# Gates and lifting products by rows, a compressor with moving weights, and a rank for the work beside the large products

## The chip, the core and the metric

The kernel runs on one core of a Trainium2 chip. The metric is the device time of one execution in microseconds (us). TensorE is PE here (its weight loads are PEld), VectorE is DVE, ScalarE is ACT, GpSimd is POOL, and SyncE is SP, which issues the loads from memory.

## What is computed

Two transformer blocks in a row on 256 tokens of width 1024, all in float32. The first block has four branches (a gated delta rule, a spatial gate, a sliding window attention, an attention over a memory), whose outputs are lifted to 1024, gated, added and projected:

```python
    ys = jnp.stack([y_a, y_b, y_c, y_m], axis=2)
    proj = jnp.einsum("btnc,ncd->btnd", ys, w_up)
    gates = jax.nn.sigmoid(gate_logits.reshape(B, T, N_BRANCH, D))
    merged = jnp.sum(gates * proj, axis=2)
    out = merged @ w_out
    return x + _rmsnorm(out, norm_post)
```

The second block has two layers. Each adds half a gated FFN (hidden size 2816), a mixer (MLA in layer 0, NSA in layer 1) and another half FFN, each behind an RMS norm of its own. The NSA mixer has a compressor: keys and values of 15 overlapping blocks of 32 tokens, in 4 groups, go through a small two-layer net.

```python
def compress_blocks(x, blk_idx, pos_emb, w1, w2):
    blocks = x[:, blk_idx] + pos_emb[None, None, :, None, :]
    flat = jnp.moveaxis(blocks, 3, 2).reshape(B, n_cmp, x.shape[2], L * x.shape[3])
    return jax.nn.gelu(flat @ w1) @ w2
```

## The kernel before

Tokens stand in two tiles of 128, called t = 0 and t = 1. Every large product is made of three fp32r matmuls: both factors are split into a high and a low part (`wh`, `wl` for weights, `xTh`, `xTl` or `yTh`, `yTl` for activations), and high x high, high x low and low x high are added in one PSUM bank. `mm3` (L236) issues the three. Weights come from memory as `raw` (SP, L211 and L214), and ACT and DVE split them (L220, L221).

There are two forms. In `ts` and `Product` (L308, L269) a 128 x 128 block of x stands in PE and the weights move, 512 columns at a time; the output has tokens as its rows. In `ws` (L315) a block of weights stands and x moves, 256 columns (all tokens) at a time; the output has features as its rows, which is the layout that a following product wants. `ws2` (L329) is a variant used by the FFNs. A factor whose rows are tokens has to be transposed first: `split_T` (L400) queues transposes on PE (L394) and the split of their result on ACT and DVE (L415, L416).

The small work is spread between the large matmuls. Transposes stand in a list `pending`, and attention, the delta rule and the compressor are generators in a list `beside`. After every large matmul `drip()` (L147) calls `step()` (L151), which issues one item of either. `wait` or `lag` items of nothing ahead of a norm's transposes (`LAG_NORM` = 28, `LAG_HIDDEN` = 20) leave time for the norm, whose own chain (square on ACT, two POOL operations for `rstd`, `xn` on DVE at L441) is written under `high_priority(100)`.

The order on each engine isn't the order of the code. The framework's scheduler takes instructions by priority, which is their place in the code minus the offset of a `high_priority` around them, among those that are ready in a timing of its own. Engines then execute their lists in order.

The merge stage (L1043 to L1085) runs the four branches one after the other. For each branch and each half of the 1024 columns, a `ws` product makes the gate (tanh on ACT, L1070) and a `ws` product lifts the branch; DVE multiplies and adds into `merged`, whose rows are features, and in the last branch `split` writes the high and low parts `moT` directly. `w_out` is then a `Product` on `moT`, and its evacuation ends in the norm that feeds the first FFN.

The compressor (L1491 to L1541) handles K and then V. It loads w1 as one tile of 1 MB, adds the position embedding (L1508), and issues 16 matmuls with w1 standing and 60 columns moving (L1513); then gelu and a second layer (L1528 and after), which gives `kcT` and `vbd` for the attention over compressed blocks.

Of the kernel before, what the change touches and what calls it, by code (L numbers as in the profile page):

```python
# [17 lines left out]
P = 128  # L18
# [75 lines left out]
def two_blocks_kernel(ctx: ExitStack, tc: tile.TileContext, a, cst_dram, cst2_dram, out):  # L94
# [51 lines left out]

    def drip():  # L147
        for _ in range(pace[0]):
            step()

    def step():  # L151
        f = pending.pop(0) if pending else None
        if f:
            f()
        elif beside:
            g = beside.pop(0)
            try:
                next(g)
                beside.append(g)
            except StopIteration:  # L160
                pass

    def idle(n):
        for _ in range(n):
            yield
# [362 lines left out]
    def first(nxt):  # L528
# [516 lines left out]
        merged = pg.tile([P, 8, T], F32)  # L1045
# [9 lines left out]
        for at, (br, name) in enumerate([(1, "b"), (2, "c"), (0, "a"), (3, "m")]):  # L1055
# [11 lines left out]
            for n in range(2):  # L1067
                gate = pg.tile([P, 4, T], F32, name="gate", bufs=1)
                ws(xT, 8, w_in, 0, 5896 + br * D + n * 512, 512,
                   lambda j0, w, pv, gate=gate: sc.activation(gate[:, j0:j0 + w, :], pv, AF.Tanh, scale=0.5))  # L1070
                if at == 3:
                    moT.append(ypair())

                def ev(j0, w, pv, n=n, gate=gate, at=at):
                    g, m = gate[:, j0:j0 + w, :], merged[:, 4 * n + j0:4 * n + j0 + w, :]
                    if at == 0:
                        ve.scalar_tensor_tensor(m, g, 1.0, pv, op0=OP.add, op1=OP.mult)
                    else:
                        ve.scalar_tensor_tensor(g, g, 1.0, pv, op0=OP.add, op1=OP.mult)
# [25 lines left out]
        in_turns([(pr, u) for u in range(4)], await_second=False)  # L1105
# [312 lines left out]
    def nsa(xn, nxt, skew):  # L1418
# [72 lines left out]
        def compress():  # L1491
            for which in range(2):
                s = "kv"[which]
                w1 = pk.tile([P, 16, P], F32, name="w1")
                nc.sync.dma_start(w1, a[f"nsa_cmp_w1_{s}_2"][0].rearrange("(k p) n -> p k n", p=P))
                w2 = pk.tile([P, P], F32, name="w2" + s)
                for b in range(2):
                    nc.sync.dma_start(w2[:, b * 64:(b + 1) * 64], a[f"nsa_cmp_w2_{s}_2"][0])
                pos = pk.tile([16, P], F32, name="pos" + s)
                nc.sync.dma_start(pos, a[f"nsa_cmp_pos_{s}_2"][0].rearrange("(j b) d -> j (b d)", b=2))  # L1500
                ps = tr()
                pe.transpose(ps[:, :16], pos, ident[:16, :16])
                posT = pk.tile([P, 16], F32, name="posT" + s)
                ve.tensor_copy(posT, ps[:, :16])
                c2 = c2s[which]
                fl = pk.tile([P, 16, 60], F32, name="flat")
                for j in range(16):
                    ve.tensor_scalar(fl[:, j, :].rearrange("p (g n) -> p g n", g=4), c2[:, :, 2 * j:2 * j + 225:16],  # L1508
                                     posT[:, j:j + 1], None, op0=OP.add)
                yield from idle(4)  # L1510
                ps = po()
                for j in range(16):
# [3 lines left out]
                hx = pk.tile([P, 60], F32, name="hx", bufs=2)  # L1516
                ve.tensor_copy(hx, ps[:, :60])
                hd = pk.tile([P, 4, 4, 32], F32, name="hid")
                gp.memset(hd, 0.0)
                h2 = pk.tile([P, 60], F32, name="h2", bufs=2)  # L1520
                gelu2(h2, hx, pk, 64)
                ve.tensor_scalar(hd[:, :, :, 0:15],
                                 h2.rearrange("p (g n) -> p g n", g=4)[:, :, None, :].to_broadcast([P, 4, 4, 15]),
                                 0.5, None, op0=OP.mult)
                yield from idle(16)
                ps = po()
                if which == 0:
                    pe.matmul(ps[:, :P].rearrange("p (g n) -> p g n", g=4), w2, hd[:, :, 0, :], start=True, stop=True)  # L1528
                    for b in range(2):
                        bs = slice(64 * b, 64 * b + 64)  # L1530
                        ve.tensor_copy(kcT[bs, :, b, 0:15], ps[bs, :P].rearrange("p (g n) -> p g n", g=4)[:, :, 0:15])
                else:
                    for g in range(4):
                        pe.matmul(ps[:, g * 64:(g + 1) * 64], hd[:, g].rearrange("p r n -> p (r n)"), w2[:, 0:64],
                                  start=True, stop=True)
# [212 lines left out]
```

## Time and profile before

| what | value |
|---|---|
| median of 3 runs | 1414.67 us (1414.62 to 1415.38) |
| profiled execution | 1415.39 us, span 1413.6 us |
| granted TensorE clock, mean | 0.999 |
| PE busy | 1387.0 us (98%) |
| PEld busy | 1208.0 us (85%) |
| DVE busy | 927.3 us (66%) |
| ACT busy | 733.3 us (52%) |
| POOL busy | 45.8 us (3%) |

A busy time is the time in which an engine has at least one instruction in work. Matmuls overlap in the pipeline of PE, so the length of a record is longer than the distance from one start to the next; what PE pays for a matmul is that distance. The stages follow each other: the first block's branches until some 250 us, its merge stage until some 396, FFN 0a until 595, MLA until 700, FFN 0b until 890, FFN 1a until 1075, NSA until 1225, FFN 1b until the end.

### The profile page before, as it was taken

The page shows a single profiled execution, that of the slowest core. Times are in us where ns is not written, and L with a number is a line of the kernel's source. Part 1 is how long each engine was busy: PE and PEld are TensorE (multiplying, and loading weights), DVE is VectorE, ACT ScalarE, POOL GpSimd, SP SyncE. Part 2 cuts the span into 40 slices and gives each one's busy share as a digit, 9 for nine tenths or more (in the row PEclk, how much of TensorE's full clock was granted, in tenths as well). Part 3 has the DMA queues.
Part 4 walks back from the last instruction along what each step waited for, and adds up shares of the span by engine and source line. Part 5 has one row for each costly group of instructions (what it writes and reads, how often), then busy time and mean ns, then how long its engine had stood idle before and what let it go on. Part 6 is the DMA issues. An engine that isn't in the chain of part 4 may idle for free.

```text
span 1413.6 us, 21329 instructions
## 1 busy us (share of the span) xinstructions
PE 1387.0 (98%) x8528; PEld 1208.0 (85%) x8528; DVE 927.3 (66%) x1587; ACT 733.3 (52%) x1293; POOL 45.8 (3%) x87
## 2 busy tenths in 40 slices
PE   7999999999999999999999999999999999999998
PEld 6998989999978888888788888888888887788886
DVE  6878666555667665669666656666665687576654
ACT  6646454343445454567454545555445467464543
POOL 1003000000010000010000000000000000000000
PEclk9999999999999999999999999999999999999999
DMA  7425634455556565533477664666556730465651
GB/s 259 149 83 166 222 126 150 149 179 180 179 164 208 182 202 183 174 116 122 140 229 258 197 208 150 200 202 197 190 188 207 203 80 31 134 207 182 200 186 60
DMA packets 172537, 241.77 MB, mean 171 GB/s; under 512 B 5264, under 2 KB 121749, under 8 KB 172309
## 3 DMA queue, kind: packets, MB, share of 16 engines
q1 hardware_dynamic: 172436, 240.40, 53.3%
q8 instruction: 67, 1.10, 0.3%
q14 instruction: 34, 0.27, 0.1%
HBM read 239.31 MB, written 4.22 MB: 172 GB/s over the span
## 4 chain that ended last, share of the span: by engine, by line
PE 86%; DMA 4%; ACT 4%; DVE 3%; POOL 1%; issue 1%; SPq 0%; POOLq 0%; ACTq 0%; DVEq 0%
PE acc L347 17%; PE acc L241 10%; PE acc L237 10%; PE acc L239 10%; PE acc L350 9%; PE d L241 5%; PE d L237 5%; PE d L239 5%; PE tr L394 4%; DVE wl L221 2%; ACT wh L220 1%; DMA raw<-in_ffn_b_w_gate_dram 1%; ACT pr L1582 1%; PE po L789 1%; DMA raw<-in_ffn_b_w_up_dram 1%
## 5 line engine op out<-in xcount | busy, mean ns | idle before, releaser
L221 DVE TENSOR_TENSOR wl<-raw,wh 128x1024 fp32r<-128x1024 f32 (+5 forms) x434 | 509.7, 1197 | 224.7 <-ACT wh L220 222.9
L220 ACT CAST wh<-raw 128x1024 fp32r<-128x1024 f32 (+5 forms) x434 | 433.8, 1029 | 308.0 <-PE d L241 95.1
L347 PE MATMUL acc<-xT,wh 128*128 128x512 f32 x1152 | 399.0, 397 | 1.5 <-DVE up L355 1.5
L350 PE MATMUL acc<-xT,wl 128*128 128x256 f32 x1152 | 298.9, 280 | 0.0
L347 PEld LDWEIGHTS acc<-xT,wh 128*128 128x128 f32 x1152 | 208.1, 188 | 43.4 <-DVE up L355 2.3
L350 PEld LDWEIGHTS acc<-xT,wl 128*128 128x128 f32 x1152 | 217.1, 188 | 12.1
L239 PE MATMUL acc<-xT,wh 128*128 128x256 f32 x544 | 156.6, 288 | 0.0
L241 PE MATMUL acc<-xT,wl 128*128 128x256 f32 x544 | 156.3, 287 | 0.0
L237 PE MATMUL acc<-xT,wh 128*128 128x256 f32 x544 | 156.1, 287 | 0.0
L241 PE MATMUL d<-wh,yTl 128*128 128x512 f32 x352 | 138.0, 392 | 0.0
L237 PE MATMUL d<-wh,yTh 128*128 128x512 f32 x352 | 137.6, 391 | 0.0
L239 PE MATMUL d<-wl,yTh 128*128 128x512 f32 x352 | 137.5, 391 | 0.0
L239 PEld LDWEIGHTS acc<-xT,wh 128*128 128x128 f32 x544 | 104.2, 192 | 1.1 <-issue 0.8
L237 PEld LDWEIGHTS acc<-xT,wh 128*128 128x128 f32 x544 | 104.2, 191 | 0.7 <-DVE y_b L481 0.3
L241 PEld LDWEIGHTS acc<-xT,wl 128*128 128x128 f32 x544 | 104.2, 191 | 0.4 <-issue 0.2
L237 PE MATMUL acc<-wh,xT 128*128 128x512 f32 (+4 forms) x256 | 97.4, 381 | 0.3 <-ACT xT L415 0.3
L239 PE MATMUL acc<-wl,xT 128*128 128x512 f32 (+4 forms) x256 | 96.2, 376 | 0.0
L241 PE MATMUL acc<-wh,xT 128*128 128x512 f32 (+4 forms) x256 | 96.0, 377 | 0.0
L241 PEld LDWEIGHTS d<-wh,yTl 128*128 128x128 f32 x352 | 66.1, 188 | 14.9 <-DVE yTl L1151 0.8
L239 PEld LDWEIGHTS d<-wl,yTh 128*128 128x128 f32 x352 | 66.1, 188 | 14.1
L237 PEld LDWEIGHTS d<-wh,yTh 128*128 128x128 f32 x352 | 66.1, 188 | 13.1
L354 ACT COPY sg<-acc 128x256 f32<-128x256 f32 x72 | 26.8, 373 | 89.2 <-PE acc L347 88.7
(436 smaller groups left out, 2034.6 us busy)
## 6 DMA issues: line engine op xcount, KB each, us to landing
raw<-in_w_in_dram SPq DMA_DIRECT2D x37, 1024.0 KB, 5.2
raw<-in_ffn_a_w_gate_dram SPq DMA_DIRECT2D x22, 1024.0 KB, 5.3
raw<-in_ffn_a_w_up_dram SPq DMA_DIRECT2D x22, 1024.0 KB, 5.3
raw<-in_ffn_a_w_down_dram SPq DMA_DIRECT2D x22, 1024.0 KB, 5.0
raw<-in_ffn_b_w_gate_dram SPq DMA_DIRECT2D x22, 1024.0 KB, 5.3
raw<-in_ffn_b_w_up_dram SPq DMA_DIRECT2D x22, 1024.0 KB, 5.3
raw<-in_ffn_b_w_down_dram SPq DMA_DIRECT2D x22, 1024.0 KB, 5.0
raw<-in_w_up_dram SPq DMA_DIRECT2D x8, 1024.0 KB, 5.0
```

Of the source, the lines that this page charges most:

```text
L220: sc.copy(h[:, c], raw[:, c])
L221: ve.tensor_sub(l[:, c], raw[:, c], f32(h[:, c]))
L237: pe.matmul(ps, ah, bh, start=start, stop=False)
L239: pe.matmul(ps, ah, bl, start=False, stop=False)
L241: pe.matmul(ps, al, bh, start=False, stop=stop)
L347: pe.matmul(ps, h[:, k, js], pair.both(kk), start=k == 0, stop=k == nk - 1)
L350: pe.matmul(ps[:, :T], l[:, k, js], pair[0][:, kk, :], start=False, stop=False)
L354: sc.copy(d, ps[:, T:])
L394: pe.transpose(box[0][:m, b * P:(b + 1) * P], src(b), ident)
L789: pe.matmul(p[:, h * 64:(h + 1) * 64], Em[:, h, :], Vs[t][:, h, :], start=True, stop=True)
L1582: sc.activation(p[:, sl], p[:, sl], AF.Exp, bias=nm[:, e:e + 1], scale=-1.0, accum_out=sm[:, e:e + 1])
```

## The change

It has three parts. `step()` runs under `high_priority(offset=60)`, so each small instruction that it issues ranks 60 places ahead of where the code has it. The merge's gates and lifting products use `ts` instead of `ws`: `merged` has tokens as its rows, and in the last branch it goes through `split_T`, with its transposes on PE; `w_out` waits for them (`await_second` is left at True). The compressor treats K and V together: its input stands (64 columns, 4 groups of 16) and w1 moves, 128 wide, K into the lower and V into the upper half of the rows of one bank; w1 comes in four chunks for each of K and V, from two buffers each; gelu is done once for both, and one transpose of `h2` gives the second layer's inputs.

```diff
+    rank = [60]
...
     def step():
-        f = pending.pop(0) if pending else None
-        if f:
-            f()
-        elif beside:
...
+        with tc.high_priority(offset=rank[0]):
+            f = pending.pop(0) if pending else None
+            if f:
+                f()
+            elif beside:
...
-        merged = pg.tile([P, 8, T], F32)
+        merged = pg.tile([P, 2, D], F32)
...
-                gate = pg.tile([P, 4, T], F32, name="gate", bufs=1)
-                ws(xT, 8, w_in, 0, 5896 + br * D + n * 512, 512,
-                   lambda j0, w, pv, gate=gate: sc.activation(gate[:, j0:j0 + w, :], pv, AF.Tanh, scale=0.5))
+                gate = pg.tile([P, 2, 512], F32, name="gate", bufs=1)
+                ts(xT, 8, w_in, 0, 5896 + br * D + n * 512, 512,
+                   lambda t, p, gate=gate: sc.activation(gate[:, t, :], p, AF.Tanh, scale=0.5))
...
-                        split(m, [v[:, j0:j0 + w, :] for v in moT[n]])
-
-                ws(yT, 4, a["w_up"][0, br], 0, n * 512, 512, ev)
+                        split_T(m, 4, [moT[n]], t, wait=LAG_HIDDEN)
+
+                ts(yT, 4, a["w_up"][0, br], 0, n * 512, 512, ev)
...
-                mo = merged.rearrange("p k t -> p (k t)")[:, t * D + m * 512:t * D + (m + 1) * 512]
+                mo = merged[:, t, ns]
...
-        in_turns([(pr, u) for u in range(4)], await_second=False)
+        in_turns([(pr, u) for u in range(4)])
...
-                w1 = pk.tile([P, 16, P], F32, name="w1")
-                nc.sync.dma_start(w1, a[f"nsa_cmp_w1_{s}_2"][0].rearrange("(k p) n -> p k n", p=P))
...
-                for j in range(16):
-                    pe.matmul(ps[:, :60], w1[:, j, :], fl[:, j, :], start=j == 0, stop=j == 15)
-                    if j % 2:
-                        yield
...
+            hidden = po()
+            for j0 in range(0, 16, 4):
+                w1, fl = [], []
+                for which in range(2):
+                    x = "kv"[which]
+                    w1.append(pk.tile([P, 4, P], F32, name="w1" + x, bufs=2))
+                    nc.sync.dma_start(w1[which], a[f"nsa_cmp_w1_{x}_2"][0, j0 * P:(j0 + 4) * P].rearrange(
+                        "(k p) n -> p k n", p=P))
...
                 yield from idle(4)
...
+                for i in range(4):
+                    for which in range(2):
+                        pe.matmul(hidden[64 * which:64 * which + 64, :P], fl[which][:, i].rearrange("p g n -> p (g n)"),
+                                  w1[which][:, i, :], start=j0 + i == 0, stop=j0 + i == 15)
+                    yield
...
+            gelu2(h2, hx, pk, P)
+            yield from idle(16)
+            ps = tr()
+            pe.transpose(ps[:, :P], h2, ident)
+            hk = pk.tile([P, 64], F32, name="hk")
+            ve.tensor_scalar(hk, ps[:, 0:64], 0.5, None, op0=OP.mult)
```

In the instruction lists this shows as follows. Up to the merge, a line of the kernel before stands 3 lines further down in the changed one (L394 becomes L397, L237 becomes L240).

The first place is PE at the end of FFN 0a. `d_4348` (before) and `d_3792` (after) are the two banks whose end starts the norm of token tile 0, and `tr<-cst,xn` are the transposes of its result. Before, with all but the first and the last of the 29 matmuls in between left out:

```order
L241 MATMUL d_4348<-wh,yTl 128x512
L237 MATMUL d_4349<-wh,yTh 128x512
...
L239 MATMUL d_4350<-wl,yTh 128x512
L394 MATMUL tr<-cst,xn 128x128
L241 MATMUL d_4350<-wh,yTl 128x512
L394 MATMUL tr<-cst,xn 128x128
L237 MATMUL d_4350<-wh,yTh 128x512
```

After, with 12 matmuls in between, of which the first and the last are shown:

```order
L244 MATMUL d_3792<-wh,yTl 128x512
L240 MATMUL d_3793<-wh,yTh 128x512
...
L244 MATMUL d_3794<-wh,yTl 128x512
L397 MATMUL tr<-cst,xn 128x128 x4
L240 MATMUL d_3793<-wh,yTh 128x512
L397 MATMUL tr<-cst,xn 128x128 x4
L242 MATMUL d_3793<-wl,yTh 128x512
```

The transposes have moved 17 matmuls ahead and stand in two groups of four.

The second place is PE at the end of the merge, where the last lifting product passes into `w_out` (banks `po`). Before:

```order
L239 MATMUL acc<-yTl,wh 128x256
L241 MATMUL acc<-yTh,wl 128x256
L237 MATMUL po<-wh,yTh 128x512
L239 MATMUL po<-wl,yTh 128x512
L241 MATMUL po<-wh,yTl 128x512
```

After:

```order
L244 MATMUL acc<-wh,yTl 128x512
L397 MATMUL tr<-cst,merged 128x128 x4
L240 MATMUL po<-wh,yTh 128x512
L242 MATMUL po<-wl,yTh 128x512
L244 MATMUL po<-wh,yTl 128x512
L240 MATMUL po<-wh,yTh 128x512
L242 MATMUL po<-wl,yTh 128x512
L397 MATMUL tr<-cst,merged 128x128 x4
```

The lifting matmuls are 512 wide, and the two groups of transposes of `merged` stand inside the first matmuls of `w_out`; two more groups stand in the same way after the first half.

The third place is SP in front of NSA's last products, where the chunks of w1 are queued. Before:

```order
L211 DMA raw<-in_nsa_w_o_dram 64x2x1024 x3
L1495 DMA w_10502<-in_nsa_cmp_w_v_dram 128x16x128
L211 DMA raw<-in_nsa_w_o_dram 64x2x1024 x5
L214 DMA raw<-in_ffn_b_w_gate_dram 128x4x512 x2
L214 DMA raw<-in_ffn_b_w_up_dram 128x4x512 x2
```

After:

```order
L214 DMA raw<-in_nsa_w_o_dram 64x2x1024 x3
L1515 DMA w1k<-in_nsa_cmp_w_k_dram 128x4x128
L1515 DMA w1v<-in_nsa_cmp_w_v_dram 128x4x128
L1515 DMA w1k<-in_nsa_cmp_w_k_dram 128x4x128
L1515 DMA w1v<-in_nsa_cmp_w_v_dram 128x4x128
L214 DMA raw<-in_nsa_w_o_dram 64x2x1024 x5
```

Chunks 2 and 3 of K and V stand where the load of V's w1 stood; chunks 0 and 1 are loaded in FFN 0b.

## Rows read from the trace of the kernel before

**Rows 1.** The page: busy time of each engine; the granted clock in 40 slices.

```profile
PE 1387.0 (98%) x8528; PEld 1208.0 (85%) x8528; DVE 927.3 (66%) x1587; ACT 733.3 (52%) x1293; POOL 45.8 (3%) x87
...
PEclk9999999999999999999999999999999999999999
```

**Rows 2.** PE's waits: line, releaser; us in total, times, longest us.

```profile
PE tr L394 <- DVE xn L441: 13.3, 6, 8.8
PE acc L347 <- DVE up L355: 1.5, 2, 1.3
```

**Rows 3.** Busy time by window, the merge stage: length, PE, PEld, DVE, ACT, POOL, clock, DMA.

```profile
250.00:396.00 146.00, 146.00 (x1169) 143.75 (x1168) 81.68 (x86) 61.59 (x74) 0.00 (x0) 1.00 0.55 174
```

**Rows 4.** Timeline of PE (start, length): 256-wide and 512-wide matmuls.

```profile
255.02 0.28 PE L237 MATMUL acc<-xT,wh 128*128 128x256 f32 x1
...
261.98 0.28 PE L239 MATMUL acc<-xT,wh 128*128 128x256 f32 x1
...
155.26 0.39 PE L241 MATMUL acc<-wh,xT 128*128 128x512 f32 x1
...
165.47 0.39 PE L241 MATMUL acc<-wh,xT 128*128 128x512 f32 x1
```

**Rows 5.** Timeline of PE at NSA's end: transposes of `xn` in groups of four.

```profile
1226.47 0.63 PE L394 MATMUL tr<-cst,xn 128*128 128x128 f32 x4 [1.03 <-DVE xn L441]
...
1227.17 0.60 PE L394 MATMUL tr<-cst,xn 128*128 128x128 f32 x4
```

**Rows 6.** Timeline of PE: the compressor's V, and the attention's pairs with 64-column weights.

```profile
1129.15 3.68 PE L1513 MATMUL wo<-flat,w 128*128 128x60 f32 x32
...
1147.39 0.44 PE L1600 MATMUL wo<-pT,vs 128*64 128x128 f32 x4 [0.16 <-ACT pT L504]
...
1147.98 0.30 PE L1622 MATMUL mm<-kcT,qT 128*128 128x32 f32 x1
```

**Rows 7.** SP's load of V's w1, and DMA issues (KB each, us to landing).

```profile
1121.52 0.74 SPq L1495 DMA_DIRECT2D w<-in_nsa_cmp_w_v_dram  x1
...
w<-in_nsa_cmp_w_v_dram SPq DMA_DIRECT2D x1, 0.5 KB, 6.9
```

**Rows 8.** Timeline at the end of FFN 0a: the norm's chain and its transposes.

```profile
585.27 0.39 PE L241 MATMUL d<-wh,yTl 128*128 128x512 f32 x1
...
585.69 0.69 DVE L1170 SCALAR_TENSOR_TENSOR res<-d,res 128x512 f32<-128x512 f32 x1 [2.03 <-PE d L241]
...
586.48 0.63 ACT L371 ACTIVATE junk<-res 128x512 bf16<-128x512 f32 x1 [2.00 <-DVE res L1170]
...
587.30 0.30 POOL L376 TENSOR_SCALAR rstd<-ss 128x1 f32<-128x1 f32 x1 [171.99 <-ACT junk L371]
...
588.27 1.42 DVE L441 SCALAR_TENSOR_TENSOR xn<-res,rstd,gain 128x512 f32<-128x512 f32 x2 [1.89 <-POOL rstd L377]
...
592.08 0.27 PE L394 MATMUL tr<-cst,xn 128*128 128x128 f32 x1
...
592.42 0.27 PE L394 MATMUL tr<-cst,xn 128*128 128x128 f32 x1
```

**Rows 9.** Timeline of PE: first transposes of `xn` behind `w_out` (twice) and MLA.

```profile
405.30 0.44 PE L394 MATMUL tr<-cst,xn 128*128 128x128 f32 x2 [1.06 <-DVE xn L441]
...
416.24 0.30 PE L394 MATMUL tr<-cst,xn 128*128 128x128 f32 x1 [0.73 <-DVE xn L441]
...
702.12 1.29 PE L394 MATMUL tr<-cst,xn 128*128 128x128 f32 x8 [0.89 <-DVE xn L441]
```

**Rows 10.** Timeline at the spatial gate: its first `vn`, and its first matmul.

```profile
128.48 0.75 DVE L864 SCALAR_TENSOR_TENSOR vn<-vn,rstd,gmn 128x512 f32<-128x512 f32 x1
...
130.10 0.27 PE L868 MATMUL mm<-vn,wsT 128*128 128x128 f32 x1
```

**Rows 11.** Busy time by window in NSA's and MLA's attention (columns as in rows 3).

```profile
1152.00:1164.00 12.00, 11.93 (x104) 9.02 (x102) 10.18 (x54) 9.22 (x31) 0.00 (x0) 1.00 0.26 88
636.00:656.00 20.00, 20.00 (x151) 16.25 (x150) 18.79 (x54) 13.63 (x43) 0.29 (x1) 1.00 0.33 106
```

More of the change, by code (lines that the diff above doesn't have):

```diff
@@ L151, in step @@
     def step():
-        f = pending.pop(0) if pending else None
-        if f:
-            f()
-        elif beside:
[L156 to L161, printed above, removed]
+        with tc.high_priority(offset=rank[0]):
[3 more added lines that the diff above has]
+            elif beside:
+                g = beside.pop(0)
+                try:
+                    next(g)
+                    beside.append(g)
+                except StopIteration:
+                    pass
     def idle(n):
@@ L1516, in compress @@
[L1516 to L1535, printed above, removed]
-                    for r in range(4):
-                        rs = slice(32 * r, 32 * r + 32)
-                        ve.tensor_copy(vbd[rs, :, r % 2, r // 2, :], ps[rs, :256].rearrange("p (g n) -> p g n", g=4))
+                posT.append(pk.tile([P, 16], F32, name="posT" + x))
@@ new lines, in compress @@
+                ve.tensor_copy(posT[which], ps[:, :16])
+            yield from idle(4)
+            hidden = po()
+            for j0 in range(0, 16, 4):
+                w1, fl = [], []
+                for which in range(2):
+                    x = "kv"[which]
+                    w1.append(pk.tile([P, 4, P], F32, name="w1" + x, bufs=2))
+                    nc.sync.dma_start(w1[which], a[f"nsa_cmp_w1_{x}_2"][0, j0 * P:(j0 + 4) * P].rearrange(
+                        "(k p) n -> p k n", p=P))
+                    f = pk.tile([P, 4, 4, 16], F32, name="flat" + x, bufs=2)
+                    fl.append(f)
+                    gp.memset(f[:, :, :, 15:16], 0.0)
+                    for i in range(4):
+                        j = j0 + i
+                        ve.tensor_scalar(f[:, i, :, 0:15], c2s[which][:, :, 2 * j:2 * j + 225:16],
+                                         posT[which][:, j:j + 1], None, op0=OP.add)
+                yield from idle(4)
+                for i in range(4):
+                    for which in range(2):
+                        pe.matmul(hidden[64 * which:64 * which + 64, :P], fl[which][:, i].rearrange("p g n -> p (g n)"),
+                                  w1[which][:, i, :], start=j0 + i == 0, stop=j0 + i == 15)
+                    yield
@@ new lines, in compress @@
+            ps = hidden
+            hx = pk.tile([P, P], F32, name="hx")
+            ve.tensor_copy(hx, ps[:, :P])
+            h2 = pk.tile([P, P], F32, name="h2")
+            gelu2(h2, hx, pk, P)
[4 more added lines that the diff above has]
+            ve.tensor_scalar(hk, ps[:, 0:64], 0.5, None, op0=OP.mult)
+            hd = pk.tile([P, 4, 4, 32], F32, name="hid")
+            gp.memset(hd, 0.0)
@@ new lines, in compress @@
+            ve.tensor_scalar(hd[:, :, :, 0:16],
+                             ps[:, 64:P].rearrange("p (g n) -> p g n", g=4)[:, :, None, :].to_broadcast([P, 4, 4, 16]),
+                             0.5, None, op0=OP.mult)
+            yield from idle(8)
+            ps = po()
+            pe.matmul(ps[:, 0:64], w2[0], hk, start=True, stop=True)
+            for b in range(2):
+                bs = slice(64 * b, 64 * b + 64)
+                ve.tensor_copy(kcT[bs, :, b, 0:15], ps[bs, 0:64].rearrange("p (g n) -> p g n", g=4)[:, :, 0:15])
@@ L1540, in nsa @@
+            ps = po()
+            for g in range(4):
+                pe.matmul(ps[:, g * 64:(g + 1) * 64], hd[:, g].rearrange("p r n -> p (r n)"), w2[1][:, 0:64],
+                          start=True, stop=True)
+            for r in range(4):
+                rs = slice(32 * r, 32 * r + 32)
+                ve.tensor_copy(vbd[rs, :, r % 2, r // 2, :], ps[rs, :256].rearrange("p (g n) -> p g n", g=4))
+            yield
         cmp = launch(compress())
```

26 lines of the change are left out of this document (9 added, 17 removed).

## The prediction

> **What bounds the kernel now.** I read the page's busy times first, then the waits of PE, then busy time by stage. PE is busy 1387.0 of 1413.6 us, at the full clock in all 40 slices, so the kernel runs at 2.4 GHz throughout [rows 1]. DVE and ACT are far below that. The two costliest waits of PE are 13.3 us before transposes of `xn`, of which 8.8 are the one at the start of the kernel, and 1.5 us before a bank of an FFN [rows 2]. In the merge stage PE is busy for all of the 146.00 us shown [rows 3]. So the end is set by what PE has to issue, plus the few waits in which it stands. Both parts of the change act on these two sums: the rewritten products take PE work away, and the rank moves small PE work earlier, closer to the work that feeds it. PE takes its instructions in the listed order, so a transpose that stands too early holds every large matmul behind it.
>
> **Gates and lifting products.** A 256-wide matmul starts 0.1200 us after the one before (255.02 to 261.98, 58 steps); a 512-wide one 0.2269 us (155.26 to 165.47, 45 steps) [rows 4]. The code has 8 rounds (4 branches, 2 halves) of 8 + 4 blocks of K, 4 column blocks, 3 terms: 1152 matmuls of 256. By rows it is 2 token tiles instead of 4 column blocks: 576 of 512. 1152 x 0.1200 = 138.2; 576 x 0.2269 = 130.7; **-7.6 us**, all on PE's path since PE has no gap there. An error of 0.001 in the wider pitch would be 0.6. The casts that feed it are the same and have room. The Trainium skill says otherwise: its page "TensorE: Matmul & The Clock Gate", section "Back-to-back issue gap", gives an isolated gap of N/2.4 + 2.5 ns, so 109 and 216 ns, by which this gain would be an estimated 1.5 us. These rows differ from it by 11 ns in both widths, and the rows decide.
>
> **Transposes of `merged`.** By rows, the last branch's sum must be transposed: 16 new transposes, in four groups of 4 on PE. A group of 4 and the 512-wide matmul behind it take 0.70 us (1226.47 to 1227.17) [rows 5], so a group costs 0.70 - 0.23 = 0.47: **+1.9 us**. The first group of a half has 12 matmuls of the other token tile ahead of it (2.7 us), its second tile's group 1.6 us; the chain between is one DVE product (about 0.7 us), one addition and no POOL, so I charge no wait there (up to +0.6 if it is late). The Trainium skill, same page, section "Part 4: PE-mode transpose", measures about 275 ns for one in a kernel; the records are as long, but they overlap, and the pitch counts. By the page's duration as a pitch it would be an estimated +4.4.
>
> **Compressor.** Before, 32 fp32 matmuls of 60 columns, two records each; the 32 records of V stand in 3.68 us, the last one's own length of 0.28 included, so 31 steps of 0.110 [rows 6]. After, 64 stationary columns and 128 moving, in two halves of a bank. The nearest row is the attention's pair with 64-column weights: 8 records in 0.59 us (1147.39 to 1147.98), 0.074 [rows 6]. 64 x (0.110 - 0.074) = -2.3. One more transpose is +0.1; the second layer is as long as before. The chain h2, hk, second layer is covered by fewer large matmuls: +0.4. The four chunks of w1 have two buffers; chunks 2 and 3 are queued on SP behind the third load of `nsa_w_o`, and can go only when chunk 0 is used. Before, the load of the V weights was issued at 1121.52 and landed 6.9 us later [rows 7]. In the new order some 5 us of PE work lie between chunk 0's last matmul and chunk 2's first; a quarter of the bytes should land in less than 6.9. I take +0.5 (0 to +2). Sum **-1.3** (-2.2 to +1).
>
> **The rank.** Only two things about it cost or pay. (a) The order alternates large and small matmuls on PE 290 times before, 195 after. An alternated transpose costs 0.34 - 0.23 = 0.11 (592.08 to 592.42) [rows 8], one in a group 0.47 / 4 = 0.12: nothing to gain beside 512-wide matmuls, a little beside 256-wide ones. **-0.5** (0 to -1.5). The wait of the FFN bank [rows 2] may go with the new order: **-0.5** (0 to -1.5).
>
> (b) **The transposes of normed rows.** At the end of an FFN the chain is: last down matmul of the tile (starts 585.27, its slot ends 585.50), `res` on DVE 585.69, square on ACT 586.48, two POOL steps from 587.30, `xn` on DVE from 588.27, two of 0.71, the first ready at 588.98 [rows 8]. That is 3.5 us after the trigger. Before, 29 matmuls stand between, 29 x 0.227 = 6.6 us, so the first transpose at 592.08 had 3 us to spare [rows 8]. After, 12 stand between: 2.7 us. PE will reach the transposes 0.8 us too early and stand: +0.9 with the semaphore. The scheduler's own clock evidently takes this chain, with its POOL steps, for shorter than it is: wherever it already put these transposes at the first moment it thought possible, PE waited: 1.06, 0.73, 0.89 and 1.03 us [rows 5, 9].
> Counted in the same way (cover before, cover after, us): token tile 0 of FFN 0a, 0b and 1a, 6.6 to 2.7, three times +0.9; token tile 1 of 0b and 1a, 6.7 and 6.2 to 2.7, whose chain is longer, +1.4 and +1.0; of 0a, 4.6 to 3.3, +0.4; MLA's two, 3.4 to 2.7 and 4.1 to 3.6, +0.7 and +0.5; NSA's two, 3.4 to 2.7, +0.7, and 3.2 to 3.9, which returns 0.7 of the 1.03 seen; `w_out`'s first unchanged at 7.5, its second, 8.5 to 7.0, +1.5. Sum 2.7 + 2.4 + 0.4 + 1.2 + 0 + 1.5 = **+8.2 us** (bounds 0 and +10).
> (c) The spatial gate's matmuls move about 4 us of PE work ahead. Before, they start at 130.10, 0.87 after the first `vn` (128.48 + 0.75) [rows 10], behind POOL steps too. DVE's order moves `vn` up part of the way: **+1.7** (0 to +3).
> (d) NSA's attention starts 3.9 us later against the large products (it waits for the compressor) and ends 2.7 earlier, so some 80 us of it are squeezed by 6.5. DVE is 10.18 of 12 us busy there; MLA ran at 18.79 of 20 with no PE gap [rows 11]. So it should fit: **+0.5** (0 to +4).
> Casts lose places on DVE and ACT to the small work; DVE at two thirds of the span hides that, at a cost of one cast (1.2 us) if not.
>
> **Sum.** -7.6 + 1.9 - 1.3 - 0.5 - 0.5 + 8.2 + 1.7 + 0.5 = +2.4. From the profiled execution (1415.39 us, 0.7 above the median of 1414.67) to 1417.8; against the median about **1417.0**. Since two of the waits are taken near their upper ends, I say **1416.5**: no difference that can be told. About 0.2%, 2.8 us, is what a measurement of this kernel can tell, so "same" is 1411.8 to 1417.5.
>
> **Rivals.**
> *The norm waits do not come.* The POOL steps or the chain run ahead of the other work better than in the rows, and transposes that come early feed the next product early. Against it: four waits of the same kind stand in the rows [rows 5, 9], and PE holds its order. Then 8.2 is lost from the sum: **1408.5**, faster. Chance 0.22.
> *DVE binds NSA's attention.* The squeeze of 6.5 us in 80 needs DVE at over 90% for long; from the point where a stretch passes MLA's 94% [rows 11] each PE product waits for a softmax. Price up to +4 with chunk 2 of w1 late by up to 2 more: 1416.5 + 4.5, **1421**, slower. Chance 0.22.
> *The width buys nothing.* If x stationary with moving weights were paced by loading weights or by casts, the 7.6 is missing: **1424**. The rows show both widths with equal loads of weights per matmul and no gap, so 0.04. The page's rule above (gain 1.5, time 1422.5) would be a mild form, and falls with the same rows.
> *Forecast* (1411.8 to 1420, half of it below 1416.5): 0.52.
>
> **Chances and range.** Faster: the first rival and a little of the forecast's lower tail, 0.24. Same: 0.41, the forecast up to 1417.5. Slower: the rest of the forecast (0.09), the second and third rival, 0.35. Range 1408 to 1421.5, which leaves out most of the third rival and the far ends of the others.
>
> **What would show it.** In the changed kernel: in the merge stage a pitch of 0.227 us and PE without gaps, the stage 6 us shorter; waits of PE before transposes of `xn` at some 20 us instead of 13.3, in ten or more pieces of 0.5 to 2.2; each with POOL's `rstd` as the late step; compressor records at 0.07 to 0.08. The prediction is wrong if those waits stay at 13 us (then it is faster), or if PE waits behind `w1` or `pr` for microseconds (then slower).

## The result, and the profile after

The changed kernel takes 1426.20 us (median of 4 runs, 1425.84 to 1427.71) against 1414.64 of the kernel before in the same comparison: a ratio of 1.0082, with a 95% interval of 1.0067 to 1.0097. It is slower by 11.6 us. The prediction had said 1416.5 with a range of 1408 to 1421.5, so the change costs more than the range allowed.

The profiled execution took 1426.41 us, with a span of 1424.6 (before: 1413.6). These are the page's busy times of the changed kernel, the line that answers to [rows 1]:

```profile
PE 1388.3 (97%) x7969; PEld 1178.3 (83%) x7969; DVE 924.9 (65%) x1583; ACT 733.9 (52%) x1291; POOL 43.4 (3%) x94
```

PE has 559 instructions fewer and is busy 1.3 us longer. The rest of the 11 us is time in which PE stands: 36.3 us of the span instead of 26.6. PE's costliest waits (line, releaser; us in total, times, longest us) answer to [rows 2]:

```profile
PE tr L397 <- DVE xn L444: 18.8, 14, 8.9
PE acc L350 <- DVE sg L358: 2.6, 4, 1.0
PE mm L871 <- DVE vn L867: 1.3, 1, 1.3
PE tr L397 <- ACT pT L507: 1.0, 2, 0.7
```

Waits for a normed row are 14 instead of 6, the spatial gate's `vn` is a new one, and the FFN's bank wait, which the prediction let go, has grown.

In the merge stage the matmuls run as predicted: 9 steps from 299.68 to 301.72 are 0.2267 each (timeline of PE, answers to [rows 4]), and PE is busy without a gap there (windows of the changed kernel, as [rows 3]):

```profile
299.68 0.39 PE L242 MATMUL acc<-wl,xT 128*128 128x512 f32 x1
...
301.72 0.40 PE L242 MATMUL acc<-wl,xT 128*128 128x512 f32 x1
```

```profile
253.40:398.60 145.20, 145.20 (x652) 119.64 (x651) 83.61 (x88) 64.61 (x79) 0.87 (x2) 1.00 0.54 178
```

The table follows the same instruction through several kernels: its start in the kernel before, and how much later (or earlier, negative) it starts in the others. "No rank" is the changed kernel without the bracket in `step()` (experiment e5).

| instruction | before, us | after | by rows alone (e3) | compressor alone (e4) | no rank (e5) |
|---|---|---|---|---|---|
| first gate (ACT) | 250.7 | +2.69 | -2.13 | +0.66 | -2.78 |
| first `res` of `w_out` (DVE) | 400.0 | -1.32 | -5.30 | +0.65 | -5.98 |
| first latent of MLA (DVE) | 604.0 | +0.65 | -6.72 | +0.92 | -7.15 |
| first `res` of MLA (DVE) | 683.5 | +3.15 | -6.75 | +0.91 | -7.22 |
| first silu product of FFN 1a's later columns (DVE) | 912.4 | +6.50 | -6.01 | +0.21 | -6.29 |
| last `res` of FFN 1a (DVE) | 1071.5 | +6.87 | -4.81 | +0.13 | -5.10 |
| last `res` of NSA (DVE) | 1222.9 | +9.47 | -5.25 | -0.32 | -5.71 |
| last `res` of FFN 1b (DVE) | 1407.0 | +10.91 | -4.68 | -0.30 | -4.18 |

Without the rank the same products are 7 us ahead at MLA. Against them (the last column) the changed kernel is 5.5 us late at the first gate and 4.7 at the first `res` of `w_out`; then it loses 3.1 up to MLA's first latent, 2.6 in MLA, 2.4 up to FFN 1a's later columns and 3.2 in NSA. FFN 1a's end gives 0.8 back, FFN 1b costs nothing.

### The profile page after: what moved, and what is told of

Read it like the earlier page. It is cut to its first block, busy times and chain, and to the rows that moved or that the text cites. A ratio compares the mean times of both kernels' runs of the same rounds, so it can differ in the third digit from the quotient of the medians.

```text
span 1424.6 us, 20246 instructions
## 1 busy us (share of the span) xinstructions
PE 1388.3 (97%) x7969; PEld 1178.3 (83%) x7969; DVE 924.9 (65%) x1583; ACT 733.9 (52%) x1291; POOL 43.4 (3%) x94
## 4 chain that ended last, share of the span: by engine, by line
PE 80%; DVE 7%; DMA 5%; ACT 4%; issue 2%; POOL 2%; SPq 0%; POOLq 0%; ACTq 0%; DVEq 0%
PE acc L350 16%; PE acc L244 8%; PE acc L242 8%; PE acc L240 8%; PE acc L353 8%; PE d L244 5%; PE d L240 5%; PE d L242 5%; PE tr L397 4%; DVE wl L224 3%; ACT wh L223 2%; DMA raw<-in_w_in_dram 1%; ACT junk L374 1%; DMA raw<-in_ffn_a_w_down_dram 1%; DMA raw<-in_ffn_b_w_up_dram 1%
## 5 line engine op out<-in xcount | busy, mean ns | idle before, releaser
L353 PE MATMUL acc<-xT,wl 128*128 128x256 f32 x1152 | 298.0, 279 | 0.0
L350 PEld LDWEIGHTS acc<-xT,wh 128*128 128x128 f32 x1152 | 207.6, 188 | 45.3 <-DVE sg L358 4.5
L353 PEld LDWEIGHTS acc<-xT,wl 128*128 128x128 f32 x1152 | 217.1, 188 | 12.3
L240 PE MATMUL acc<-wh,xT 128*128 128x512 f32 (+4 forms) x384 | 147.2, 383 | 0.5 <-ACT xT L418 0.5
L242 PE MATMUL acc<-wl,xT 128*128 128x512 f32 (+4 forms) x384 | 147.3, 384 | 0.0
L244 PE MATMUL acc<-wh,xT 128*128 128x512 f32 (+4 forms) x384 | 146.0, 381 | 0.0
L240 PE MATMUL d<-wh,yTh 128*128 128x512 f32 x352 | 137.4, 390 | 0.0
L240 PEld LDWEIGHTS acc<-wh,xT 128*128 128x128 f32 x384 | 73.1, 190 | 13.4 <-ACT xT L418 0.9
L242 PEld LDWEIGHTS acc<-wl,xT 128*128 128x128 f32 x384 | 73.1, 190 | 12.6
L244 PE MATMUL acc<-xT,wl 128*128 128x256 f32 x288 | 83.1, 289 | 0.0
L244 PEld LDWEIGHTS acc<-wh,xT 128*128 128x128 f32 x384 | 72.9, 190 | 12.3
L240 PE MATMUL acc<-xT,wh 128*128 128x256 f32 x288 | 82.8, 288 | 0.0
L242 PE MATMUL acc<-xT,wh 128*128 128x256 f32 x288 | 82.6, 287 | 0.0
L240 PEld LDWEIGHTS d<-wh,yTh 128*128 128x128 f32 x352 | 66.1, 188 | 12.9
```

The source lines that it names most:

```text
L240: pe.matmul(ps, ah, bh, start=start, stop=False)
L242: pe.matmul(ps, ah, bl, start=False, stop=False)
L244: pe.matmul(ps, al, bh, start=False, stop=stop)
L350: pe.matmul(ps, h[:, k, js], pair.both(kk), start=k == 0, stop=k == nk - 1)
L353: pe.matmul(ps[:, :T], l[:, k, js], pair[0][:, kk, :], start=False, stop=False)
```

## The experiments

All ratios and medians are against runs of the kernel before on the same chip; its medians were 1415.26 to 1415.73 us.

### The parts one by one: e1 to e4

**e1**: the changed kernel with

```diff
-    rank = [60]
+    rank = [0]
```

> The changed kernel with rank 0: the products by rows and the new compressor stay, the small work ranks by its place in the code again. Theory R (the rank alone makes the kernel slower; the rewritten products gain what the sum of the prediction gave, -7.6 +1.9 -1.3): about 1407.5 us, and PE's waits before transposes of xn back at 13 to 14 us. Rival M (the rewritten products lose, through the transposes of merged or a pitch over 0.227): 1415 or more. Rival C (the two parts only hurt together): 1407 here, and the rank alone on the kernel before costs under 5.

**e2**: the kernel before with the bracket alone

```diff
+    rank = [60]
...
+        with tc.high_priority(offset=rank[0]):
```

> The kernel before with the rank alone: every small instruction of step() ranks 60 higher. Theory R: 1414.6 + 15 to 20 = 1430 to 1434 us. Of that the norm's transposes give 8 (the prediction's term), the attention stages of MLA and NSA, where small matmuls now stand in rows of their own, some 6 to 8. Rival M: under 1417. Rival C: under 1420.

**e3**: the kernel before with the merge alone

```diff
-                ws(xT, 8, w_in, 0, 5896 + br * D + n * 512, 512,
...
+                ts(xT, 8, w_in, 0, 5896 + br * D + n * 512, 512,
...
-                        split(m, [v[:, j0:j0 + w, :] for v in moT[n]])
+                        split_T(m, 4, [moT[n]], t, wait=LAG_HIDDEN)
```

> The kernel before with the gates and lifting products by rows alone. By the prediction's terms -7.6 + 1.9 = -5.7, about 1409 us; by theory R the same; by rival M 1414 or more.

**e4**: the kernel before with the compressor alone

```diff
-                    pe.matmul(ps[:, :60], w1[:, j, :], fl[:, j, :], start=j == 0, stop=j == 15)
...
+                        pe.matmul(hidden[64 * which:64 * which + 64, :P], fl[which][:, i].rearrange("p g n -> p (g n)"),
+                                  w1[which][:, i, :], start=j0 + i == 0, stop=j0 + i == 15)
```

> The kernel before with the new compressor alone. By the prediction's terms -2.3 + 0.5 + 0.5 = -1.3, about 1413.3 us. A rival: the chain h2, hk, second layer and the late chunks of w1 delay NSA's attention, 1415 to 1418.

| run | median, us | ratio to before (95% interval) |
|---|---|---|
| e1, rank 0 | 1417.39 | 1.0012 (1.0002 to 1.0021) |
| e2, rank alone | 1431.39 | 1.0111 (1.0095 to 1.0126) |
| e3, by rows alone | 1411.27 | 0.9965 (0.9952 to 0.9977) |
| e4, compressor alone | 1415.35 | 1.0001 (0.9992 to 1.0011) |

The rank alone costs 16 us, as theory R said. By rows alone is faster by 4.0, less than the 5.7 of the prediction's terms. The compressor alone is worth nothing that can be measured. But e1 falls on no theory's side cleanly: with rank 0 it is 2.1 us slower than the kernel before, hardly clear of the noise, and not 4 us faster. Its waits for normed rows are back, and still it loses:

```profile
PE tr L397 <- DVE xn L444: 13.1, 5, 9.2
```

In MLA e1 needs 82.60 us from the first latent to the first `res`, e3 79.45, with the same 520 matmuls (windows; the first row is of e1, the second of e3):

```profile
597.90:680.50 82.60, 80.82 (x520) 63.83 (x521) 59.54 (x170) 48.06 (x130) 5.99 (x14) 1.00 0.32 108
```

```profile
597.30:676.75 79.45, 77.82 (x520) 63.88 (x521) 59.16 (x170) 47.64 (x130) 5.96 (x14) 1.00 0.34 112
```

Either the two rewritten parts hurt each other, or the bracket does something even with offset 0. The framework's counter of places is set back when a bracket is left, so the small work inside uses up no places and everything behind it moves closer. e5 and e8 ask which.

### The bracket, and who is in it: e5 to e8

**e5**: the changed kernel with `step()` as it was before, no bracket.

```diff
-        with tc.high_priority(offset=rank[0]):
-            f = pending.pop(0) if pending else None
...
+        f = pending.pop(0) if pending else None
```

> Products by rows and new compressor, with step() as before: no high_priority around it at all. The bracket of high_priority itself gives back the places in the schedule that the small work used, so offset 0 was not the same as no bracket. Theory B (the bracket costs, even with offset 0): the two parts add up, 1411.3 + 0.1 = about 1411.4 us, 6 under the run with rank 0. Rival C (by rows and the compressor hurt each other): 1417 again.

**e6**: the bracket around queued transposes alone.

```diff
-        with tc.high_priority(offset=rank[0]):
...
+        if f:
+            with tc.high_priority(offset=rank[0]):
                 f()
```

> The changed kernel with the rank on the queued transposes alone (norms, hidden, merged), not on attention, delta rule and compressor. The PE work between each norm's trigger and its transposes is the same as in the changed kernel, by the order. If the norm's waits are the term of the prediction: 8.2 above the run without rank, 1419.6 us. Rival: the waits are smaller than that and the attention is the larger part: 1413 to 1416.

**e7**: the bracket around the generators alone.

```diff
-        with tc.high_priority(offset=rank[0]):
...
+            g = beside.pop(0)
+            with tc.high_priority(offset=rank[0]):
                 try:
```

> The changed kernel with the rank on attention, delta rule and compressor alone; the norms' transposes stand where they stood before (6.6 us behind the trigger at an FFN's end). If the rank on the small matmuls costs what is missing from the prediction: 1411.4 + 5 to 8 = 1416 to 1419 us, lost in the branches, MLA and NSA. Rival: under 1413, then the norms carry it all.

**e8**: rank 60, with the places kept.

```diff
-        with tc.high_priority(offset=rank[0]):
+        p = tc.cur_priority
+        tc.cur_priority = p - rank[0]
...
+        tc.cur_priority += rank[0]
```

> The changed kernel with rank 60, but the small work keeps its places in the count (60 is subtracted before the step and added again behind it). If giving back the places is a large part (theory B): 3 to 6 under the changed kernel, 1420 to 1423 us. If the 60 alone counts: 1426.

| run | median, us | ratio to before (95% interval) |
|---|---|---|
| e5, no rank | 1411.66 | 0.9972 (0.9960 to 0.9983) |
| e6, queued transposes ranked | 1426.55 | 1.0073 (1.0058 to 1.0088) |
| e7, generators ranked | 1415.31 | 0.9995 (0.9985 to 1.0004) |
| e8, rank 60 with places kept | 1422.34 | 1.0044 (1.0029 to 1.0059) |

e5 settles e1: without the bracket the two parts add up (1411.7), so the bracket with offset 0 costs 5.7 us by itself, and rival C falls. e8 agrees: with the places kept the same rank is 3.9 us cheaper. The rank of the changed kernel costs 1426.2 - 1411.7 = 14.5 us.

The pages show what kind of time this is. These are the lines of e5 and of e1:

```profile
PE 1381.8 (98%) x7969; PEld 1176.7 (83%) x7969; DVE 925.9 (66%) x1583; ACT 734.4 (52%) x1291; POOL 45.3 (3%) x94
```

```profile
PE 1386.9 (98%) x7969; PEld 1177.9 (83%) x7969; DVE 925.1 (65%) x1583; ACT 734.9 (52%) x1291; POOL 44.0 (3%) x94
```

With the same 7969 matmuls PE is busy 5.1 us longer in e1, and stands only 1.3 us longer (29.0 us of a span of 1415.9, against 27.7 of 1409.5). So the bracket costs by the order of the work on PE, and hardly by waits.

e7 comes out just under its expectation, +3.7. e6 went past both of its cases: +14.9, as much as the whole rank. Its loss has a part that the changed kernel doesn't have. In the groups of PE (line, engine, operation, count | busy us, mean ns), NSA's scores take 20.8 us in e6 and 13.6 in e5; the first row is of e6, the second of e5:

```profile
L1591 PE MATMUL mm<-kTs,qT 64*128 64x256 f32 x96 | 20.8, 419 | 0.1
```

```profile
L1588 PE MATMUL mm<-kTs,qT 64*128 64x256 f32 x96 | 13.6, 402 | 0.3 <-DVE rv4n L1603 0.3
```

The scores come in runs of four matmuls (8 records), each on 64 of PE's 128 rows. In e5 a run stands together and takes 1.07 us; in e6 ranked transposes stand inside it, and it takes 1.11 and 0.62. The timelines of PE, e5 first, then e6:

```profile
1152.89 1.14 PE L1588 MATMUL mm<-kTs,qT 64*128 64x256 f32 x8
1153.96 0.33 PE L394 MATMUL tr<-cst,pr 128*128 128x128 f32 x1
```

```profile
1164.88 1.13 PE L1591 MATMUL mm<-kTs,qT 64*128 64x256 f32 x6
1165.99 0.70 PE L397 MATMUL tr<-cst,pr 128*128 128x128 f32 x4
1166.62 0.70 PE L1591 MATMUL mm<-kTs,qT 64*128 64x256 f32 x2
1167.24 0.33 PE L397 MATMUL tr<-cst,pr 128*128 128x128 f32 x1
```

Two such matmuls side by side cost what one alone costs, some 0.54 us, and a transpose of the full array between them parts them. In e5 the records of such a pair start some 7 ns apart.

### The norms by themselves, and two side questions: e9 to e12

**e9**: the rank on all small work but the norms' transposes (those are marked in `norm_T`).

```diff
+        if pending and getattr(pending[0], "norm", False):
+            pending.pop(0)()
+            return
         with tc.high_priority(offset=rank[0]):
```

> The changed kernel with the rank on all small work but the norms' transposes, which stand where they stood before (the covers are 6.6 us at the FFNs' ends again). If the waits before those transposes are worth what the two traces show (11.7 us of stalls against 4.9), 1426.2 - 6.8 = 1419.4 us; by the prediction's term of 8.2, 1418.0. Rival: under 1415, then they carry everything that the rank costs.

**e10**: the rank on the norms' transposes alone.

```diff
-        with tc.high_priority(offset=rank[0]):
...
+        if getattr(f, "norm", False):
+            with tc.high_priority(offset=rank[0]):
                 f()
```

> The same the other way: by rows and the new compressor, and the rank on the norms' transposes alone. 1411.7 + 6.8 = 1418.5 us by the stalls, 1419.9 by the prediction's term. Rival: under 1415, then the waits cost little by themselves and other work fills them.

**e11**: no rank; coupled quads one behind the other.

```diff
-                    turns = zip(*[quads[g][0](s) for g, s in zip(group, banks)])
+                    gens = [quads[g][0](s) for g, s in zip(group, banks)]
+                    turns = (0 for g in gens for _ in zip(g, g)) if len(gens) == 2 else zip(*gens)
```

> No rank; in the coupled quads of MLA's and NSA's attention, the score matmuls of the two quads stand one quad behind the other instead of in turns. In NSA the partners of a pair use the two halves of PE's rows. If neighbours on different halves run side by side and others don't: 96 records of NSA's scores take 20 to 26 us instead of 12.8, and the time is 1411.7 + 7 to 13. If the place in the order is all that matters: 1412, no difference.

**e12**: by rows alone, and later transposes behind `w_out`.

```diff
-            nxt(t, 28 if t == 0 else 36)
+            nxt(t, 36 if t == 0 else 44)
```

> A candidate for the best of these: only the products by rows, no rank, the kernel before's compressor, and the transposes of w_out's two norms 8 items later (lag 36 and 44 instead of 28 and 36). The two waits there (1.32 and 0.83 us without it) should go: 1411.3 - 1.5 to 2.1 = about 1409.5 us. Rival: the first FFN then starts too late on them, no gain.

| run | median, us | ratio to before (95% interval) |
|---|---|---|
| e9, rank without the norms | 1421.07 | 1.0040 (1.0026 to 1.0054) |
| e10, rank on the norms alone | 1418.83 | 1.0025 (1.0015 to 1.0034) |
| e11, quads one behind the other | 1411.66 | 0.9973 (0.9963 to 0.9984) |
| e12, by rows, later norms | 1417.68 | 1.0014 (1.0005 to 1.0023) |

e9 and e10 put the norms' transposes at 5.1 us (1426.2 - 1421.1) and 7.2 us (1418.8 - 1411.7): the mechanism of the prediction, near its size. PE's waits for normed rows show it directly; the rows are of e5, e10 and e9 in this order:

```profile
PE tr L394 <- DVE xn L441: 11.9, 5, 8.3
```

```profile
PE tr L399 <- DVE xn L446: 19.1, 14, 8.9
```

```profile
PE tr L400 <- DVE xn L447: 13.0, 6, 8.9
```

19.1 - 11.9 = 7.2 us of waiting, and 7.2 us of time: nothing fills a wait of PE. The page of e10 says the same: PE is busy only 0.6 us longer than in e5, and stands 7.0 us longer (34.7 us of a span of 1417.1).

```profile
PE 1382.4 (98%) x7969; PEld 1176.9 (83%) x7969; DVE 926.4 (65%) x1583; ACT 734.4 (52%) x1291; POOL 45.6 (3%) x94
```

But e9 also says that the rank costs 9.4 us without the norms. That is what the prediction had not seen.

e11 came out on the side of its second expectation: the order inside a run of four doesn't matter. The records of a pair start some 14 ns apart instead of 7, so the order on PE did change, and the scores take 13.7 us, as before:

```profile
L1589 PE MATMUL mm<-kTs,qT 64*128 64x256 f32 x96 | 13.7, 402 | 0.3 <-DVE rv4n L1604 0.3
```

So partners need not be neighbours in turns; what e6 shows is that the run must not be cut by a matmul of the full array.

e12 was meant to beat e3 and lost 6.4 us to it. The waits for `xn` fell, but the first product of FFN 0a then stood for its input:

```profile
406.69 0.80 PE L241 MATMUL acc<-wh,xT 128*128 128x512 f32 x1 [4.31 <-DVE xT L416]
```

Behind this wait the granted clock, full before it, was 0.50, so 1.2 instead of 2.4 GHz (windows of e12, columns as in [rows 3]):

```profile
408.00:410.00 2.00, 2.00 (x6) 1.52 (x6) 1.16 (x3) 0.00 (x0) 1.09 (x2) 0.50 0.00 0
```

From 407.29 to 411.98 eleven 512-wide matmuls start 0.427 us apart instead of 0.227, which costs 2.2 us more. The wait and the clock together are about the 6.4 us.

Of all versions, e3 (by rows alone, 1411.27 us), e5 and e11 (both 1411.66) are the best, and can't be told apart.

### Where the rest of the rank goes: e13 and e14

**e13**: no bracket while the first block is built, the bracket elsewhere. **e14**: no bracket while MLA is built. In both, `step()` leaves the bracket out while `plain[0]` is set.

```diff
+    plain[0] = True
     first(n0)
+    plain[0] = False
```

```diff
+    plain[0] = True
     mla(n1, n2)
+    plain[0] = False
```

> The changed kernel, but step() has no bracket while the first block is built (branches, merge, w_out and its two norms, whose transposes belong to it). If the rank's cost in a stage is that stage's own, what the two traces show up to FFN 0a's first gate goes: 4.7 up to the end of w_out's first tile and 0.7 of its second norm, so 1426.2 - 5.4 = about 1421 us. If the cost moves on (later stages take up the slack): 1424 or more.

> The changed kernel, but step() has no bracket while MLA is built. If the cost is MLA's own: 1426.2 - 2.6 (between the first latent and the first output) - 0.5 to 0.9 (its two norms) = about 1423 us. If attention only takes the slack from elsewhere: 1425 or more.

| run | median, us | ratio to before (95% interval) | gained on the changed kernel |
|---|---|---|---|
| e13 | 1423.23 | 1.0054 (1.0037 to 1.0071) | 3.0 |
| e14 | 1423.24 | 1.0053 (1.0038 to 1.0068) | 3.0 |

The gains are by the medians; against each comparison's own kernel before (1414.64 and 1415.73 us) they are some 4 us each. In e14 the last `res` of MLA comes 4.8 us earlier than in the changed kernel, in e13 the first `res` of `w_out` 3.8 and MLA's first latent 4.8. In both, 1.1 to 1.2 of that is lost again in FFN 0b, and some 3.5 is left at the end. So MLA is worth about what was expected, and the first block 3 to 4, not 5.4. In the windows (length, PE, PEld, DVE, ACT, POOL) up to the first `res` of `w_out`, then to MLA's first latent, then to MLA's first `res`, the changed kernel reads

```profile
0.00:398.60 398.60, 386.15 (x2404) 340.65 (x2405) 263.10 (x415) 202.34 (x352) 16.77 (x33) 1.00 0.51 166
398.60:604.60 206.00, 201.41 (x1051) 170.91 (x1049) 134.33 (x168) 105.93 (x162) 5.75 (x12) 1.00 0.57 186
604.60:686.60 82.00, 80.34 (x520) 64.33 (x521) 58.99 (x170) 48.12 (x130) 7.06 (x14) 1.00 0.34 112
```

and e5

```profile
0.00:394.00 394.00, 384.02 (x2403) 340.74 (x2404) 262.75 (x416) 202.35 (x352) 19.13 (x33) 1.00 0.52 168
394.00:596.80 202.80, 200.76 (x1051) 170.88 (x1049) 134.41 (x168) 106.33 (x162) 7.27 (x12) 1.00 0.59 189
596.80:676.30 79.50, 77.79 (x520) 63.86 (x521) 59.17 (x171) 47.65 (x130) 5.95 (x14) 1.00 0.33 113
```

In the second stretch PE's idle time grows from 2.0 to 4.6 us, mostly by norm waits (3.8 us instead of 1.8). In MLA it doesn't grow (1.7 and 1.7): there the same 520 matmuls keep PE busy 2.55 us longer. What small matmuls cost depends on what stands beside them. A stretch of the changed kernel's PE in MLA:

```profile
644.48 0.43 PE L1372 MATMUL po<-pT,vt 128*64 128x128 f32 x2
644.84 0.70 PE L1345 MATMUL wo<-kT,qT 96*128 96x256 f32 x2
645.47 0.65 PE L1372 MATMUL po<-pT,vt 128*64 128x128 f32 x6
646.05 0.28 PE L1347 MATMUL wo<-maskb,identb 128*128 128x256 bf16 x1
646.27 0.66 PE L1372 MATMUL wo<-pT,vt 128*64 128x128 f32 x8
646.85 0.70 PE L1345 MATMUL mm<-kT,qT 96*128 96x256 f32 x2
647.39 0.27 PE L1347 MATMUL mm<-maskb,identb 128*128 128x256 bf16 x1
647.50 0.59 PE L1345 MATMUL mm<-kT,qT 96*128 96x256 f32 x2
647.94 0.27 PE L1347 MATMUL mm<-maskb,identb 128*128 128x256 bf16 x1
```

The two records of a score take 0.44 us between two masks (647.50 to 647.94), 0.54 behind `pT,vt`, which uses half of PE's columns (646.85 to 647.39), and 0.63 between two of those (644.84 to 645.47). In addition `pT,vt`, whose matmuls pair up on the two halves of the columns, stands in a run of 2 and one of 6 instead of one of 8. A run of 8 takes 0.58 us (646.27 to 646.85); the two take 0.36 (644.48 to 644.84) and 0.58 (645.47 to 646.05), so the cut costs 0.36. It is e6's effect once more. In e5 and e14 all 12 runs of MLA are whole; three are cut in the changed kernel.

Added up over MLA, from each start to the next, the scores take 1.6 us more than in e5 (12.0 and 10.4), `pT,vt` 1.1 more (8.1 and 7.1) and the transposes 0.9; the large matmuls give 1.05 back. No run measured the change of shape around the scores by itself.

## Why the prediction was wrong

**PE bounds the kernel: right.** In e10, 7.2 us more of waiting were 7.2 us more of time. The granted clock of the changed kernel is 0.999 in the mean, as before.

**Gates and lifting products, -7.6, and transposes of `merged`, +1.9: right in the stage, wrong at the end.** The pitch is 0.2267 us (0.2269 was taken from [rows 4]), and PE has no gap. e3 is 5.3 us ahead at the first `res` of `w_out`, where -5.7 was predicted, and 6.7 at MLA's first latent, since a bank wait of 1.3 us in FFN 0a has gone. It ends only 4.0 ahead. The prediction took it that what PE gains in a stage stays gained. It doesn't: PE waits for FFN banks in places where the kernel before had slack. Behind MLA these waits are 2.1 us in e3 and 3.2 in e5, against 0.3 before, and behind MLA e3 loses 2.1 us of its lead and e5 3.0. One of them can be followed back to a cast that waits for a load of `w_down`. In e5, ACT stands 1.89 us for a load at 916.47, and PE 1.10 us for the bank behind it:

```profile
916.47 1.05 ACT L220 CAST wh<-raw 128x1024 fp32r<-128x1024 f32 x1 [1.89 <-DMA raw<-in_ffn_a_w_down_dram]
```

```profile
920.90 0.50 PE L347 MATMUL acc<-xT,wh 128*128 128x512 f32 x1 [1.10 <-DVE sg L355]
```

In the kernel before, the same cast stood 0.72 us for its load, and PE did not wait:

```profile
921.55 1.06 ACT L220 CAST wh<-raw 128x1024 fp32r<-128x1024 f32 x1 [0.72 <-DMA raw<-in_ffn_a_w_down_dram]
```

The load was issued 6.4 us ahead of its cast in e5 (910.04) and 5.1 before (916.43). Why it takes longer to land there stays open. The term "FFN bank wait, -0.5" had the wrong sign: the wait is 2.6 to 3.8 us in most of the kernels with rewritten products, against 1.5 [rows 2], but 0.6 to 1.4 in e7, e8 and e11.

**Compressor, -1.3: less in NSA, nothing at the end.** From FFN 1a's last `res` to NSA's last, e4 gains 0.5 us, and its median doesn't differ from before; where the rest goes was not separated. The pitch was estimated well: the two of a pair start together and the pairs 0.109 us apart, so 0.054 for a record in a run (timeline of the changed kernel), with cuts in the runs that raise the mean to 0.08.

```profile
1126.27 0.27 PE L1527 MATMUL wo<-w1v,flatv 128*64 128x128 f32 x1
1126.28 0.27 PE L1527 MATMUL wo<-w1k,flatk 128*64 128x128 f32 x1
1126.38 0.27 PE L1527 MATMUL wo<-w1v,flatv 128*64 128x128 f32 x1
```

**Transposes of normed rows, +8.2: right, a little too large.** e10 measures 7.2, e9 5.1. The waits in total are 18.8 us, 5.5 more than before and 6.9 more than in e5. They stand where the prediction put them, but at FFN ends they are 0.7 and 0.8 to 0.9 instead of its 0.9 and 1.0 to 1.4, and MLA's two are 0.73 and 0.42 where one of 0.89 stood before (timeline of the changed kernel: token tile 0 of FFN 0a, 0b and 1a, then tile 1 of 0b and 1a; [rows 8] had no wait there):

```profile
588.17 0.55 PE L397 MATMUL tr<-cst,xn 128*128 128x128 f32 x3 [0.71 <-DVE xn L444]
...
883.00 0.55 PE L397 MATMUL tr<-cst,xn 128*128 128x128 f32 x3 [0.71 <-DVE xn L444]
...
1071.71 0.55 PE L397 MATMUL tr<-cst,xn 128*128 128x128 f32 x3 [0.72 <-DVE xn L444]
...
893.18 0.63 PE L397 MATMUL tr<-cst,xn 128*128 128x128 f32 x4 [0.89 <-DVE xn L444]
...
1081.81 0.63 PE L397 MATMUL tr<-cst,xn 128*128 128x128 f32 x4 [0.81 <-DVE xn L444]
```

**The spatial gate, +1.7: near.** PE waits 1.33 us there, with `vn` late as predicted (128.95; [rows 10] had none):

```profile
128.95 1.16 PE L871 MATMUL mm<-vn,wsT 128*128 128x128 f32 x8 [1.33 <-DVE vn L867]
```

**"Only two things about it cost or pay": the step that failed.** The prediction priced the rank by the waits that the order lets one foresee, and let everything else move at no cost: alternations -0.5, attention +0.5. Apart from the norms that is 1.2 us with the spatial gate and the FFN bank; e9 measures 9.4. Two things were missing. First, the bracket isn't only an offset. It gives back the places that the small work used, so even offset 0 changes the order on PE, at 5.7 us (e1 against e5), and rank 60 with its places kept is 3.9 us cheaper than the change (e8). The diff says rank 60, and the prediction took it at its word. Second, the order of the small matmuls on PE isn't free. The prediction went by the count of alternations, which fell from 290 to 195, and took fewer of them for neutral or a gain, because groups of transposes cost as much as alternated ones [rows 5, 8]. That holds for transposes beside 512-wide matmuls. For attention's matmuls, which use parts of the array, MLA got 2.5 us slower with the same instructions and no new waits. Nor is the count what decides: counted in the same way it is 300 in e5 and 321 in e1, and e1 is busy 5.1 us longer. What e1 and the changed kernel share in MLA are cut runs of `pT,vt`: 16 and 15 runs instead of 12.

**The sum.** The rank was to cost 9.4 and costs 14.5; the rewritten products were to give 7.0 and give 3.0 (e5 against the first comparison's 1414.64) to 3.8 (against its own). These two misses, 5.1 and 3.2 to 4.0, are about the distance from 1417.0 to 1426.2. Between the profiled executions of e5 and the changed kernel the rank costs 15.1 us of span: PE is busy 6.5 longer (1381.8 and 1388.3, the same 7969 matmuls) and stands 8.6 longer (27.7 and 36.3). The standing is above all the norms' (e10: 7.0), the busy time comes from the order on PE, as in e1 (5.1), and the prediction had that at nothing. By stages, taking the bracket away gives back 3 to 4 us in the first block (e13) and as much in MLA with its norms (e14); of the 3.2 us in NSA 1.5 are waits for `xn`. The FFNs were not separated.

**The rivals.** The one that forecast no norm waits is refuted by e10 (its 1408.5 is 1408.3 by its own terms, 1416.5 - 8.2). "DVE binds NSA's attention" named the right direction (1421, slower) by luck: DVE's busy time is the same, and no wait of PE in NSA exceeds 0.3 us for `pr` and 0.7 for its transposed `pT`; e6 shows that NSA can lose 6.8 us by the order on PE (157.6 us from FFN 1a's last `res` to NSA's, 150.8 in e5). "The width buys nothing" is refuted by e3.

## What to carry to other kernels

Where one engine is busy 98% of the time, don't expect a higher rank for the small work to pay: here it brought nothing, and the transposes that reached PE ahead of their input cost their whole lateness (e10). If a few transposes already wait at the first moment that the scheduler allows, expect that more rank puts others there too. Keep matmuls that pair up on halves of the array in whole runs. Before changing an order by a bracket or a rank, run the bracket with offset 0 as well: here it cost 5.7 us on its own. Matmuls of equal work are cheaper wide (0.227 us for 512 columns against 2 x 0.120), but expect later stages to hand back part of the gain where a cast already waits for its load (0.72 us in the kernel before).

## What the runs showed of the hardware

Two fp32 matmuls on 64 rows of PE, or on 64 columns, run side by side when they stand in one run of such matmuls: four scores in 1.07 us, but 1.11 and 0.62 when cut into three and one by transposes of the full array (e6); eight records of `pT,vt` in 0.58, but 0.36 and 0.58 when cut into two and six (MLA's stretch above). They don't have to stand in turns (e11). The Trainium skill, page "TensorE: Matmul & The Clock Gate", section "Part 3: Packing small matmuls — row/col tiling", says that tiles of the array run concurrently; the rows agree (pairs start some 7 ns apart in e5), and in e6 a full-array matmul between the partners ends it.

A score of 96 rows costs 0.44 us between masks of the full array and 0.63 between matmuls of 64 columns, so changing the shape of the array that is in use costs up to 0.2 us on PE with no wait shown (MLA's stretch above); this is a reading of one trace, and no run tested it by itself.

After PE had stood 4.31 us, its granted clock was 0.50, and 512-wide matmuls started 0.427 us apart instead of 0.227 (e12).
